# Alternating the C batches of a state-space layer between VectorE and GpSimd, with a second product buffer

## The chip, the cores and the metric

The kernel runs on one core of one Trainium2 chip. The metric is the device time of one execution in microseconds; of several runs the median is taken. The engines are TensorE (PE, with its weight loads PEld), VectorE (DVE), ScalarE (ACT), GpSimd (POOL) and SyncE (SP). SP, ACT and POOL can also start DMAs.

## The reference, cut to what matters

One layer of a trunk over 512 latent tokens (width 1024) with 256 context tokens. A normalised and modulated input goes through one wide projection, whose parts feed a short convolution (`xa`, `xb`, `cg`), a bidirectional S5 state-space layer (`u`) and a neighbourhood attention (`q`, `k`, `v`); sigmoid gates (`ga`, `gb`, `gc`) merge the three, and a squared-ReLU MLP follows. The change lies in the preparation of the state-space layer:

```python
lam_bar = jnp.exp(lam_dt)
b_bar = ((lam_bar - 1.0) / lam)[..., None] * lax.complex(b_re, b_im)
c_mat = lax.complex(c_re, c_im)
h_f = diag_scan(lam_bar[0], s5_drive(ux, b_bar[0])) + ...
y = jnp.real(einsum('blgp,gnp->blgn', h_f, c_mat[0]) + einsum('blgp,gnp->blgn', h_b, c_mat[1]))
```

The kernel runs the scan in chunks of 8 tokens. For that it needs the input matrices times the powers of `lam_bar` (called E here) and the output matrices times the powers of `lam_bar` (called CA here). Both are products of complex numbers, formed for 32 groups in 8 batches of 4 groups.

## The kernel before, in words

**The weights.** `UNITS` lists the work of TensorE: first `xa` 0 to 3, `cg` 0 to 3, `xb` 0 to 3, `uc` 0 to 3 (the context's part of `u`), then gates and the convolution's output, and so on to the MLP. `slot(i)` emits one unit. For it a weight block is loaded (`raw`, issued by SP), split into two parts that together hold float32 (`wh` by ScalarE at L173, `wl` by VectorE at L176), multiplied in 24 matmuls (L99 to L101, `mm3`), and evacuated from PSUM by `ev_unit` in the slot after. The PSUM tag `m` has three buffers, so an evacuation that is late stops TensorE some units later. The evacuation of `cg` is L950 to L953 (one ScalarE and five VectorE instructions), that of `xb` is L956 (VectorE, reads PSUM), L92 (ScalarE) and L93 (VectorE), that of `uc` is a ScalarE copy and two DMAs.

**The preparation beside it.** Each slot calls `pump()` twice, and `pump` advances every generator in `gens` by one step:

- `gen_s5e` forms E, all on GpSimd: for each batch `b` two times two products (`prod`, L422) and a sum (L458, L467). TensorE then uses the batch twice: `lags` multiplies it with C (tile `kps`), `turned` transposes it (tile `etps`); ScalarE copies the transposed batch to `et` (L445) and issues its DMA to `E_d` (L446). The batch's inputs `bc` are loaded by a DMA that ScalarE issues (L429).
- `gen_s5c` forms CA: for each batch four products (L422) and two sums (L499), then a DMA by SP to `C_d` (L501). The inputs `cb` (two buffers) are loaded by a DMA that ScalarE issues (L491). Batches 0 to 4 are VectorE's, 5 to 7 GpSimd's. `c1` (the result) and `tc` (the second product) have one buffer each, so a batch's first write of `c1` waits for the DMA of the batch before.

`gen_s5c` begins when the context's generator is done, and its pool takes the memory that the context used. When both preparations are emitted and the units have come to `ga`, these pools are given back, and `S5B` takes their memory: it loads `et`, `ca` and `ks` from DRAM and runs the scan on TensorE, VectorE, GpSimd and ScalarE between the gates' units.

**The order.** Each engine and each DMA queue runs its instructions in a fixed order. That order is laid out when the kernel is built, by a planner that goes by the program's order and by its own estimate of when each instruction could start; an instruction that waits holds everything behind it on its engine.

Of the kernel before, what the change touches and what calls it, by code (L numbers as in the profile page):

```python
# [9 lines left out]
F32 = mybir.dt.float32  # L10
# [65 lines left out]
def trunk(tc, xT, ctxT, cond, condT, vecs, wst, s5p, s5bc, dmat, biasA, outT):  # L76
# [3 lines left out]
    V, S, P, PE = nc.vector, nc.scalar, nc.gpsimd, nc.tensor  # L80
# [23 lines left out]
    with es:  # L104
# [11 lines left out]
        def pa(name):  # L116
            return pp.tile([128, 1024], F32, tag="a", bufs=2, name=name)
# [300 lines left out]
        def prod(eng, out, mat, cf, b):  # L418
            shp = [128, 4, 8, 16]
            m4 = mat[:, :, None, :].to_broadcast(shp)  # L420
            c4 = s5["CF"][cf][:, 4 * b:4 * b + 4, :, None].to_broadcast(shp)
            eng.tensor_tensor(out.rearrange("p (g s n) -> p g s n", g=4, s=8), m4, c4, op=MUL)  # L422

        def gen_s5e(pool):
            kev = pool.tile([128, 2, G, 16], F32, name="kev")

            def loadbc(b):
                t = pool.tile([128, 512], F32, tag="bc", bufs=2, name=f"bc{b}")
                nc.scalar.dma_start(t[:, 0:384], s5bc[b][:, 0:384])  # L429
                return t  # L430

            def lags(b, e1, cm):
                kps = pa(f"kps{b}")[:, :128].rearrange("p (g m) -> p g m", g=4)
                for g in range(4):
                    for c in range(2):
                        PE.matmul(kps[:, g], e1[:, c, 128 * g:128 * g + 128], cm[:, 4 * c + g], start=c == 0, stop=c == 1)
                S.copy(kev[:, :, 4 * b:4 * b + 4].rearrange("p e g m -> p g e m"), kps.rearrange("p g (e m) -> p g e m", e=2))

            def turned(b, e1):
                ps = pa(f"etps{b}").rearrange("p (a m) -> p a m", a=8)  # L440
                for g in range(4):
                    for c in range(2):
                        PE.transpose(ps[:, 2 * g + c], e1[:, c, 128 * g:128 * g + 128], ident)
                et = pool.tile([128, 8, 128], F32, tag="et", bufs=1, name=f"et{b}")
                S.copy(et, ps)  # L445
                nc.scalar.dma_start(E_d[b], et)  # L446

            bc, old = loadbc(0), None
            for b in range(9):
                if b < 8:  # L450
                    nxt = loadbc(b + 1) if b < 7 else None
                    B = bc[:, 0:128].rearrange("p (c g n) -> p c g n", c=2, g=4)
                    cm = bc[:, 128:384].rearrange("p (a m) -> p a m", a=8)
                    e1 = pool.tile([128, 2, 512], F32, tag="e1", bufs=2, name=f"e1{b}")
                    ta = pool.tile([128, 512], F32, tag="ta", name=f"ta{b}")
                    prod(P, e1[:, 0], B[:, 0], "cr", b)
                    prod(P, ta, B[:, 1], "nci", b)
                    P.tensor_tensor(e1[:, 0], e1[:, 0], ta, op=ADD)  # L458
                    yield
                if old is not None:  # L460
                    lags(b - 1, *old)
                    yield
                if b < 8:
                    ta = pool.tile([128, 512], F32, tag="ta", name=f"tb{b}")
                    prod(P, e1[:, 1], B[:, 0], "nci", b)
                    prod(P, ta, B[:, 1], "cr", b)
                    P.tensor_tensor(e1[:, 1], e1[:, 1], ta, op=SUB)  # L467
                    yield
                if old is not None:
                    turned(b - 1, old[0])  # L470
                    yield
                old = (e1, cm)
                bc = nxt

            kf0 = pool.tile([16, G, 16], F32, tag="bc", bufs=2, name="kf0")
            dmt = pool.tile([16, G, 16], F32, tag="bc", bufs=2, name="dmt")
            nc.scalar.dma_start(dmt, dmat)
            nc.sync.dma_start(kf0, kev[112:128, 0])
            yield
            V.tensor_tensor(kf0, kf0, dmt, op=ADD)  # L480
            V.tensor_tensor(kev[0:16, 1], kev[0:16, 1], kf0, op=ADD)
            for e, s in ((e, s) for s in range(8) for e in range(2) if e or s < 7):
                i = 16 * (7 * e + s)
                nc.sync.dma_start(KT_d[:, :, i:i + 16].rearrange("g n m -> n g m"), kev[16 * s:16 * s + 16, e])
            yield

        def gen_s5c(pool):
            for b in range(8):
                eng = V if b < 5 else P
                t = pool.tile([128, 128], F32, tag="cb", bufs=2, name=f"cb{b}")  # L490
                nc.scalar.dma_start(t, s5bc[b][:, 384:512])  # L491
                C = t.rearrange("p (c g n) -> p c g n", c=2, g=4)
                c1 = pool.tile([128, 2, 512], F32, tag="c1", bufs=1, name=f"c1{b}")
                yield
                for c, (x, y, o) in enumerate((("ar", "ai", SUB), ("ai", "ar", ADD))):
                    ta = pool.tile([128, 512], F32, tag="tc", name=f"tc{b}{c}")
                    prod(eng, c1[:, c], C[:, 0], x, b)
                    prod(eng, ta, C[:, 1], y, b)
                    eng.tensor_tensor(c1[:, c], c1[:, c], ta, op=o)  # L499
                    yield  # L500
                nc.sync.dma_start(C_d[b], c1)  # L501
                yield
# [654 lines left out]
        stc_cm.__exit__(None, None, None)  # L1157
        s5c_cm = tc.tile_pool(name="s5c", bufs=1, side="right")
        gcc = gen_s5c(s5c_cm.__enter__())
        gens.append(gcc)  # L1160
        while ga_ in gens or gcc in gens or UNITS[i][0] != "ga":
# [306 lines left out]
```

## Time and profile before

| what | value |
|---|---|
| runs | 1035.29, 1036.31, 1037.55 us |
| median | 1036.31 us |
| the profiled execution | 1036.69 us |
| its span, first to last instruction | 1034.9 us |
| mean granted TensorE clock | 0.979 |
| busy: PE, DVE, ACT, POOL | 995.7, 577.6, 379.9, 216.0 us |

The profiled execution is 1.8 us longer than its span. TensorE is busy for 96% of the span, and the other engines for at most 56%; the shares are means over stages that differ.

### The profile page before, as it was taken

The numbers are of one execution on the slowest core, as the hardware profiler recorded it, in microseconds if no ns is written. First come the engines' busy times: TensorE is split into PE (matmuls) and PEld (weight loads), VectorE is DVE, ScalarE is ACT, GpSimd is POOL, SyncE is SP. The second block draws the span as 40 slices with busy tenths as digits, with TensorE's granted clock in tenths as the row PEclk, the third lists the DMA queues.
The fourth block names the chain that finished last, engine by engine and source line by source line (L and its number), as shares of the span: only waits on it lengthen the run. The fifth ranks groups of instructions, "written<-read, shape, count | busy, mean of one in ns | idle before, by whom it ended". The sixth has DMA issues, their size and how long they took to land.

```text
span 1034.9 us, 13596 instructions
## 1 busy us (share of the span) xinstructions
PE 995.7 (96%) x5386; PEld 818.1 (79%) x5386; DVE 577.6 (56%) x941; ACT 379.9 (37%) x611; POOL 216.0 (21%) x169
## 2 busy tenths in 40 slices
PE   7999996999899999989999999999999999999997
PEld 4468886878788787878877788998888888888887
DVE  4943799468772145666487895665432324443322
ACT  3234522432222234555465443444321213442311
POOL 3165654657751023310210200000000000000000
PEclk8999998999899999999999999999999999999999
DMA  9427335973546465433344574223232232232202
GB/s 365 172 79 214 120 127 203 237 270 127 173 161 202 156 231 219 145 136 107 122 149 148 195 256 152 82 82 123 82 120 84 82 117 87 82 123 82 82 1 82
DMA packets 64543, 149.38 MB, mean 144 GB/s; under 512 B 28864, under 2 KB 41152, under 8 KB 52064
## 3 DMA queue, kind: packets, MB, share of 16 engines
q1 hardware_dynamic: 47360, 137.90, 38.8%
q10 hardware_dynamic: 17120, 10.62, 3.6%
q8 instruction: 42, 0.69, 0.3%
q14 instruction: 21, 0.17, 0.0%
HBM read 130.16 MB, written 18.32 MB: 143 GB/s over the span
## 4 chain that ended last, share of the span: by engine, by line
PE 66%; DVE 13%; DMA 8%; POOL 6%; issue 3%; ACT 3%; ACTq 0%; SPq 0%; DVEq 0%; POOLq 0%
PE m L99 10%; PE m L100 10%; PE m L101 10%; DMA raw<-in_wst_dram 4%; DVE wl L176 2%; PE ops L840 2%; DMA C_d<-c 2%; PE wo L100 1%; PE wo L99 1%; DVE v L689 1%; PE wo L101 1%; PE st_a L515 1%; DVE fg L953 1%; POOL junk L1086 1%; PE ptps L825 1%
## 5 line engine op out<-in xcount | busy, mean ns | idle before, releaser
L176 DVE TENSOR_TENSOR wl<-raw,wh 128x1024 fp32r<-128x1024 f32 x144 | 191.1, 1327 | 219.1 <-ACT wh L173 214.4
L173 ACT CAST wh<-raw 128x1024 fp32r<-128x1024 f32 x144 | 151.0, 1049 | 299.7 <-PE m L100 151.1
L99 PE MATMUL m<-rg,wh 128*128 128x512 f32 (+1 forms) x480 | 184.2, 385 | 0.0
L101 PE MATMUL m<-rg,wl 128*128 128x512 f32 (+1 forms) x480 | 183.9, 384 | 0.0
L101 PEld LDWEIGHTS m<-rg,wl 128*128 128x128 f32 x480 | 90.1, 188 | 19.1
L99 PEld LDWEIGHTS m<-rg,wh 128*128 128x128 f32 x480 | 89.9, 188 | 18.7
L100 PE MATMUL m<-rg,wh 128*128 128x512 f32 (+1 forms) x256 | 96.4, 378 | 0.0
L1086 POOL TENSOR_TENSOR junk<-raw,silx 128x1024 f32<-128x1024 f32 x16 | 45.9, 2868 | 208.6 <-DMA raw<-in_wst_dram 207.4
L100 PE MATMUL m<-actl,wh 128*128 128x512 f32 x224 | 87.8, 392 | 0.0
L100 PEld LDWEIGHTS m<-rg,wh 128*128 128x128 f32 x256 | 48.0, 188 | 8.6
L100 PEld LDWEIGHTS m<-actl,wh 128*128 128x128 f32 x224 | 42.0, 187 | 9.8
L1041 DVE SCALAR_TENSOR_TENSOR fg<-m,mod,fg 128x512 f32<-128x512 f32 x14 | 10.5, 751 | 52.8 <-PE m L101 52.8
L515 PE MATMUL st_a<-raw,cs 128*2 128x256 f32 x128 | 33.1, 415 | 4.9 <-DMA raw<-in_wst_dram 3.9
L689 DVE TENSOR_TENSOR_SCAN v<-r,v 128x96 f32<-128x96 f32 x64 | 29.5, 524 | 14.8 <-POOL v L681 14.8
L92 ACT CAST rg<-relu 128x512 fp32r<-128x512 f32 (+1 forms) x36 | 20.3, 575 | 38.5 <-DVE relu L1034 38.5
L1090 DVE SCALAR_TENSOR_TENSOR jk<-raw,silx 128x1024 bf16<-128x1024 f32 x16 | 21.8, 1361 | 20.5 <-DMA raw<-in_wst_dram 20.5
L93 DVE TENSOR_TENSOR actl<-relu,rg 128x512 fp32r<-128x512 f32 (+1 forms) x36 | 22.3, 631 | 18.5 <-ACT rg L92 18.5
L100 PE MATMUL wo<-rg,wh 128*128 128x256 f32 (+1 forms) x104 | 31.8, 309 | 0.0
L99 PE MATMUL wo<-rg,wh 128*128 128x256 f32 (+1 forms) x104 | 31.8, 307 | 0.0
L101 PE MATMUL wo<-rg,wl 128*128 128x256 f32 (+1 forms) x104 | 31.5, 306 | 0.0
L1087 ACT ACTIVATE junk<-junk 128x1024 f32<-128x1024 f32 x16 | 17.0, 1061 | 36.4 <-POOL junk L1086 36.4
L515 PEld LDWEIGHTS st_a<-raw,cs 128*2 128x2 f32 x128 | 10.8, 90 | 24.6 <-issue 10.8
(439 smaller groups left out, 2404.3 us busy)
## 6 DMA issues: line engine op xcount, KB each, us to landing
raw<-in_wst_dram SPq DMA_DIRECT2D x94, 1024.0 KB
E_d<-et ACTq DMA_DIRECT2D x8, 512.0 KB
C_d<-c SPq DMA_DIRECT2D x8, 512.0 KB
et<-E_d SPq DMA_DIRECT2D x8, 512.0 KB
ca<-C_d SPq DMA_DIRECT2D x8, 512.0 KB
raw<-in_wst_dram SPq DMA_DIRECT2D x4, 512.0 KB
u<-U_d SPq DMA_DIRECT2D x8, 256.0 KB
ks<-KT_d SPq DMA_DIRECT2D x32, 64.0 KB
```

Of the source, the lines that this page charges most:

```text
L92: S.copy(hi, src)
L93: (eng or V).tensor_tensor(lo, src, f(hi), op=SUB)
L99: PE.matmul(ps, a[0], b[0], start=start, stop=False)
L100: PE.matmul(ps, a[0], b[1], start=False, stop=False)
L101: PE.matmul(ps, a[1], b[0], start=False, stop=stop)
L173: S.copy(a, src)
L176: V.tensor_tensor(b, src, f(a), op=SUB)
L515: PE.matmul(ps, cs[:, kt], half(h)[:, 256 * (kt % 4):256 * (kt % 4) + 256], start=kt == 0, stop=kt == 7, skip_group_check=True)
L689: V.tensor_tensor_scan(v[:, g, c], r8, v[:, g, c], 0.0, op0=MUL, op1=ADD)
L840: PE.matmul(ops[r], v[:rows, vt, r], pt[:rows, h, t], start=t == 0, stop=t == 3, skip_group_check=True)
L1086: P.tensor_tensor(junk, half(h), silx, op=MUL)
L1090: V.scalar_tensor_tensor(jk, half(h), 1.0, silx, op0=MUL, op1=MUL, accum_out=modx[:, i:i + 1])
```

## The change

Three edits, all in the preparation of the state-space layer. Batch `b` of CA goes to GpSimd where `b` is odd and to VectorE where it is even, so that each has four. `c1` and `tc` have two buffers. `et` has two buffers.

```diff
@@ gen_s5e / turned
-                et = pool.tile([128, 8, 128], F32, tag="et", bufs=1, name=f"et{b}")
+                et = pool.tile([128, 8, 128], F32, tag="et", bufs=2, name=f"et{b}")
@@ gen_s5c
-                eng = V if b < 5 else P
+                eng = P if b % 2 else V
...
-                c1 = pool.tile([128, 2, 512], F32, tag="c1", bufs=1, name=f"c1{b}")
+                c1 = pool.tile([128, 2, 512], F32, tag="c1", bufs=2, name=f"c1{b}")
...
-                    ta = pool.tile([128, 512], F32, tag="tc", name=f"tc{b}{c}")
+                    ta = pool.tile([128, 512], F32, tag="tc", bufs=2, name=f"tc{b}{c}")
```

## Rows read from the trace of the kernel before

**Rows 1.** Three stretches of 26 us: busy us (and count) of PE, PEld, DVE, ACT, POOL; clock; DMA.
```profile
130.00:156.00 26.00, 26.00 (x140) 21.75 (x139) 25.89 (x32) 6.25 (x9) 13.54 (x10) 1.00 0.41 136
156.00:182.00 26.00, 18.07 (x109) 16.41 (x108) 23.72 (x27) 7.22 (x11) 11.10 (x8) 0.88 0.56 197
182.00:208.00 26.00, 25.71 (x137) 21.87 (x137) 11.18 (x10) 10.41 (x13) 16.22 (x14) 0.99 1.03 243
```

**Rows 2.** TensorE's waits, 156 to 182 us: total us, times, longest us.
```profile
PE etps L443 <- ACT et L445: 4.0, 1, 4.0
PE uc L99 <- DVE fg L956: 1.7, 1, 1.7
PE uc L101 <- DVE wl L176: 1.6, 1, 1.6
```

**Rows 3.** VectorE in time order: start us, us, instruction, idle before it.
```profile
156.92 1.49 DVE L422 TENSOR_TENSOR c<-cb,CFar 128x512 f32<-128x512 f32 x1 [1.00 <-DMA C_d<-c]
...
176.66 0.68 DVE L956 TENSOR_TENSOR fg<-xb,fg 128x512 f32<-128x512 f32 x1
177.26 0.68 DVE L499 TENSOR_TENSOR c<-c,tc 128x512 f32<-128x512 f32 x1
```

**Rows 4.** GpSimd in time order: E, its first CA batch, the scan's first instruction.
```profile
131.42 1.46 POOL L422 TENSOR_TENSOR tb<-bc,CFcr 128x512 f32<-128x512 f32 x1
...
140.72 1.06 POOL L422 TENSOR_TENSOR ta<-bc,CFnci 128x512 f32<-128x512 f32 x1 [6.14 <-DMA bc<-in_s5bc_dram]
...
156.80 1.05 POOL L422 TENSOR_TENSOR e<-bc,CFcr 128x512 f32<-128x512 f32 x1
157.82 1.50 POOL L422 TENSOR_TENSOR e<-bc,CFnci 128x512 f32<-128x512 f32 x1
...
162.55 1.61 POOL L467 TENSOR_TENSOR e<-e,tb 128x512 f32<-128x512 f32 x1
178.07 1.92 POOL L422 TENSOR_TENSOR tc<-cb,CFai 128x512 f32<-128x512 f32 x1 [13.92 <-ACT rg L92]
...
216.73 0.21 POOL L618 IOTA iot<- 128x96 int32 x1 [3.40 <-DMA C_d<-c]
```

**Rows 5.** Groups by form, 130 to 182 us: count, busy us, mean ns, idle before.
```profile
L499 DVE TENSOR_TENSOR c<-c,tc 128x512 f32<-128x512 f32 x10 | 8.4, 836 | 0.0
L953 DVE SCALAR_TENSOR_TENSOR fg<-fg,vec,fg 128x504 f32<-128x504 f32 x6 | 7.1, 1184 | 0.0
L422 DVE TENSOR_TENSOR c<-cb,CFai 128x512 f32<-128x512 f32 x5 | 6.5, 1290 | 0.0
L422 DVE TENSOR_TENSOR tc<-cb,CFai 128x512 f32<-128x512 f32 x5 | 4.3, 852 | 0.0
L422 DVE TENSOR_TENSOR c<-cb,CFar 128x512 f32<-128x512 f32 x5 | 4.2, 844 | 1.9 <-DMA C_d<-c 1.9
L422 DVE TENSOR_TENSOR tc<-cb,CFar 128x512 f32<-128x512 f32 x5 | 4.2, 835 | 0.1
L953 DVE SCALAR_TENSOR_TENSOR fg<-fg,vec,fg 128x7 f32<-128x7 f32 x6 | 3.9, 652 | 0.0
```

**Rows 6.** VectorE's L953, 130 to 182 us: ns min/median/max of one.
```profile
L953 DVE SCALAR_TENSOR_TENSOR fg<-fg,vec,fg x12: 210/876/1767, 128.7 to 150.3; 128x504 f32<-128x504 f32 x6, 128x7 f32<-128x7 f32 x6
```

**Rows 7.** ScalarE and its DMA issues in time order.
```profile
163.05 0.34 ACTq L491 DMA_DIRECT2D cb<-in_s5bc_dram  x1
...
177.90 1.01 ACT L445 COPY et<-etps 128x1024 f32<-128x1024 f32 x1
```

**Rows 8.** TensorE in time order: `kps` of the last E batch.
```profile
171.54 0.71 PE L436 MATMUL kps<-bc,e 128*128 128x32 f32 x5 [0.61 <-issue]
```

**Rows 9.** TensorE's waits, 216 to 230 us.
```profile
PE yps L711 <- DMA ks<-KT_d: 1.8, 1, 1.8
```

**Rows 10.** Busy time in stretches of 4 us; the granted clock is third from the end.
```profile
164.00:168.00 4.00, 2.35 (x12) 2.14 (x11) 3.63 (x5) 2.13 (x3) 0.15 (x1) 0.66 0.69 268
...
180.00:184.00 4.00, 4.00 (x27) 4.00 (x26) 1.67 (x2) 1.40 (x3) 3.19 (x3) 0.70 1.00 243
```

## What the change was expected to do

> **What bounds the kernel now.** I read the page first: TensorE is busy for 996 of 1035 us, so a change off TensorE can only win back, or add to, some 39 us of idle time and what the clock loses. I then asked for the busy time of every engine in stretches of 26 us, to find where that idle time lies beside the code that changes. The CA batches lie between 130 us, after which all five of VectorE's come, and 217 us, where the scan's first instruction had waited for the last of them [rows 4, 5]. From 130 to 156 us TensorE has no gap and VectorE is busy for 25.89 of 26 us; from 156 to 182 us TensorE is idle for 26.00 - 18.07 = 7.9 us while VectorE is busy for 23.7 [rows 1]. The view of TensorE's waits says on whom: 1.7 us for an evacuation of `xb` on VectorE, 1.6 us for a weight split on VectorE, 4.0 us for the copy of `et` on ScalarE [rows 2]. That copy starts at 177.90, right behind a cast that waits for the evacuation at 176.66 [rows 3, 7]. So all three, 7.3 us, are VectorE being late. I read its line in order of time to see why: the instructions of CA stand in front of the evacuations, and some take 1.49 us that elsewhere take 0.68 [rows 3].
>
> **Why those instructions are long.** VectorE starts a CA product at 156.92, GpSimd started a product at 156.80 that takes 1.05; VectorE's ends at 158.41, 0.56 after GpSimd's end at 157.85. GpSimd's next one starts at 157.82, takes 1.50 instead of 1.06, and ends 0.9 after VectorE's [rows 3, 4]. The two take turns, a whole instruction each. The evacuations L956, which read PSUM, keep their 0.68. The Trainium skill states this in "SBUF — State Buffer", section "Who interferes with whom": a VectorE instruction with two SBUF inputs contends with a GpSimd instruction that reads SBUF, and the one that comes second waits for the whole of the first. The trace agrees: 1.49 and 1.50 us against 0.68 and 1.06 alone. By that rule at its strictest, each us of GpSimd's work paid in full, the sum below would be 15.9 - 9.1 - 1.8 = +5.0 us, as an estimate; by the busy shares of the two engines alone it would be rival A's -10.4.
>
> What GpSimd's work costs VectorE can be read from the groups. From 130 to 182 us VectorE's 30 CA instructions take 8.4 + 6.5 + 4.3 + 4.2 + 4.2 = 27.6 us [rows 5]; at 0.68 each they would take 20.4, so 7.2 are waiting. The six long L953 take 7.1 against 6 x 0.68 = 4.1 (3.0 more), the six short ones 3.9 against 6 x 0.21 = 1.3 (2.6 more) [rows 5, 6]. Together 12.8 us. GpSimd ran 14 instructions of E against them (first at 131.42, last at 162.55), at least 14 x 1.06 = 14.8 us alone [rows 4]. Each us of GpSimd's work cost VectorE 12.8 / 14.8 = 0.86 us.
>
> **The change part by part.** *Batches 1 and 3 leave VectorE.* That takes 12 instructions of 0.60 (the distance of starts, 176.66 to 177.26 [rows 3]) from its line: 7.2 us. *The second buffer of `c1`* takes away VectorE's waits for the DMA to `C_d`: 1.9 us [rows 5]. Relief: 9.1 us.
>
> *The same batches come to GpSimd* while VectorE is still full. They can't start much earlier: their memory is the context's, and VectorE's five batches all come after 130 us [rows 5]. Two batches are 12 x 1.06 = 12.7 us, which at 0.86 cost VectorE 10.9 us. The bounds are 0 (GpSimd's part falls into VectorE's pauses) and 12.7; I take 0.86, since the rows are of the same engines, forms and stretch.
>
> *The second buffer of `tc`* frees batch 5. Before, GpSimd began it at 178.07, and the row names a ScalarE cast; but what ends just then is VectorE's last sum of batch 4 (177.26 + 0.68 = 177.94), which reads the only `tc` [rows 3, 4]. With two, batch 5 follows batch 3 on GpSimd and brings its 6.4 us forward. Bounds 0 and 6.4 us; I take half, 3.2, times 0.86: 2.7 us. Batch 6 moves to VectorE later, where that engine has room (11.2 of 26 us busy from 182 to 208 [rows 1]), and costs nothing.
>
> VectorE's balance by 178 us is thus -9.1 + 10.9 + 2.7 = +4.5 us later. TensorE already waits for it, so it is late by as much: +4.5 us, with bounds of -7.3 (its three waits gone; more can't be won there) and +10.0 (all 19.1 us of three batches paid).
>
> *Batches 5 to 7 in a row become 5 and 7.* The scan's memory comes free with the last DMA to `C_d`; GpSimd's first instruction of it waits until 216.73 [rows 4]. TensorE then waits 1.8 us for `ks`, loaded behind that [rows 9]. With one batch of 6.4 us less and no wait between batches this chain ends that much earlier, and TensorE comes later, so I take the whole 1.8 us off. Bounds: 0 and 1.8.
>
> *The second `et`* gives nothing: the copy that TensorE waited for stands behind the cast and so behind the evacuation of 176.66, not behind a busy buffer. If the buffer were the cause, at most the 4.0 us of [rows 2], already inside the 7.3.
>
> *Waits that the change adds.* ScalarE issues the load of `cb` for batch b + 2 once batch b has read its own; at 163.05 it issued one just as VectorE's last product of batch 2 ended [rows 7]. For odd batches it now waits for GpSimd, and behind it on ScalarE stand the casts `rg` and `wh` that VectorE and TensorE need. SP waits likewise with the DMA to `C_d` while weight loads stand behind it. I price both at 0, since GpSimd's batch ends at about the time of the next evacuation; if they bite, they add to the same lateness, up to the 6.4 us of one batch.
>
> *Clock.* TensorE's granted clock falls to 0.66 and 0.70 in slices after its gaps [rows 10], between its levels of 2.4 and 1.2 GHz. The gaps stay, so I leave it: 0. If they went, up to (0.34 + 0.30) x 4 = 2.6 us would come back.
>
> Sum: +4.5 - 1.8 = +2.7 us on the profiled execution's 1036.7 (span 1034.9 and 1.8 around it), 1039.4; the median of the runs is 0.4 lower, so **1039 us**. A difference under 0.2%, 2 us, can't be told from none.
>
> **The rivals.** *A, VectorE is freed (faster).* If GpSimd's batches fall into pauses (it waited 6.14 us for one load of `bc` [rows 4]), or the planner moves the evacuations ahead of CA, the 7.3 us go, 1.8 at the scan, and half of the clock's 2.6: 1036.3 - 10.4 = 1026 us. It decides where GpSimd's work costs VectorE less than s, with s x (12.7 + 3.2) = 9.1 + 1.8, s = 0.69. For it speaks that 0.69 is not far below 0.86; against it, that fewer VectorE instructions do not lessen what GpSimd demands.
>
> *B, nothing to be measured.* The overlap is near 0.69 and relief and cost cancel: 1036 us.
>
> *C, GpSimd's line holds up E (slower still).* The last E batch ends at 162.55 + 1.61 = 164.2 and TensorE needs it at 171.54 [rows 4, 8], 7.4 us later. If the planner puts batches 1 and 3 in front, 12.7 us and up to 12 turns of 0.60 for VectorE come before it, 19.9 us, of which the pause of 6.14 takes up some: 13.8 - 7.4 = 6.4 us late. That gives 1039 + 6 = 1045 us. It decides where more than 7.4 us are put in front; against it, the planner puts E's own instructions first in the program.
>
> **How the numbers follow.** My forecast (1037 to 1043) has 0.40, C 0.15, A 0.29, B 0.16. Slower is the forecast and C, 0.55; same is B, 0.16; faster is A, 0.29. The range leaves out a tenth on each side: down to 1027, into A, and up to 1048, where C and the unpaid waits on ScalarE meet. The likeliest case alone is 1037 to 1043.
>
> **What would show it.** Right: from 130 to 182 us VectorE's CA instructions still average above 0.8 us, GpSimd's busy time there rises from 24.6 to over 30 us, and TensorE's idle time from 156 to 190 us grows to over 10 us, its waits still on L956, L176 and L445. The wait for `ks` at 224 us is gone. Wrong: TensorE's idle time there is under 4 us (A), or its new wait is on `kps` (C). The forecast also fails if the planner's new order opens or closes gaps in the scan (from 216 us on), which I price at nothing.

## The result, and the profile after

The changed kernel takes 1047.74 us (median of 4 runs, 1043.79 to 1053.68); beside it on the same chip the kernel before took 1036.93 (4 runs, 1035.29 to 1037.98). The ratio is 1.0106, with a 95% interval from 1.0076 to 1.0136: slower by 10.8 us. The profiled execution of after took 1047.11 us with a span of 1045.3, which is 10.4 more than before.

**Where TensorE stands still.** The first fence is the view of busy time by stretch: the three stretches of [rows 1], then four of 4 us. The second is TensorE's waits, first from 124 to 212 us (total us, times, longest us), then from 208 to 345 us, where the scan lies.

```profile
130.00:156.00 26.00, 21.50 (x104) 17.01 (x104) 26.00 (x28) 4.37 (x6) 20.23 (x15) 0.92 0.28 104
156.00:182.00 26.00, 17.69 (x75) 14.52 (x74) 24.48 (x20) 6.49 (x10) 25.32 (x17) 0.76 0.55 197
182.00:208.00 26.00, 21.30 (x138) 20.20 (x138) 14.48 (x13) 9.47 (x14) 17.98 (x13) 0.86 0.82 229
...
172.00:176.00 4.00, 0.36 (x2) 0.37 (x2) 3.18 (x4) 1.20 (x2) 4.00 (x4) 0.56 0.24 91
176.00:180.00 4.00, 4.00 (x17) 3.78 (x17) 4.00 (x3) 0.75 (x3) 4.00 (x3) 0.50 0.37 108
196.00:200.00 4.00, 2.49 (x12) 2.49 (x12) 0.00 (x0) 0.00 (x0) 2.68 (x3) 0.54 0.98 182
200.00:204.00 4.00, 4.00 (x24) 4.00 (x24) 0.00 (x0) 1.28 (x2) 1.30 (x3) 0.60 0.88 283
```

```profile
PE kps L436 <- POOL e L467: 11.9, 3, 7.6
PE xb L101 <- DVE wl L176: 2.1, 1, 2.1
PE kps L436 <- POOL e L458: 2.0, 2, 1.2
PE xb L99 <- DVE fg L950: 1.6, 1, 1.6
...
PE stps L664 <- DMA u<-U_d: 3.9, 1, 3.9
PE yps L711 <- DMA ks<-KT_d: 2.7, 4, 1.1
PE yps L713 <- POOL h L703: 1.9, 1, 1.9
```

TensorE now waits 11.9 + 2.0 = 13.9 us for E at `kps`, where before it waited for nothing but its own sequencer [rows 8]. Its waits that lead back to VectorE went from 7.3 us [rows 2] to 2.1 + 1.6 = 3.7. So the new wait is on GpSimd: the two waits on VectorE lie at 150 and 153 us, and from 156 to 208 us all of TensorE's waits, 13.0 us, are at `kps`. In all TensorE is idle for 78 - 60.49 = 17.5 us of these three stretches; before it was 8.2. The clock is the second part of the loss: in the slices after a standstill TensorE is busy all the time at a granted clock of 0.50 (which is 1.2 of 2.4 GHz) or 0.60.

**Why E is late.** GpSimd in time order (start, us, instruction, idle before it), then the two batches of `kps` on TensorE that waited longest:

```profile
127.51 1.32 POOL L422 TENSOR_TENSOR c<-cb,CFar 128x512 f32<-128x512 f32 x1 [3.65 <-DMA cb<-in_s5bc_dram]
128.79 1.49 POOL L422 TENSOR_TENSOR c<-cb,CFai 128x512 f32<-128x512 f32 x1
130.25 1.58 POOL L422 TENSOR_TENSOR e<-bc,CFcr 128x512 f32<-128x512 f32 x1
...
170.95 1.50 POOL L422 TENSOR_TENSOR c<-cb,CFar 128x512 f32<-128x512 f32 x1
172.41 1.50 POOL L422 TENSOR_TENSOR c<-cb,CFai 128x512 f32<-128x512 f32 x1
173.87 1.71 POOL L467 TENSOR_TENSOR e<-e,tb 128x512 f32<-128x512 f32 x1
...
196.20 1.26 POOL L467 TENSOR_TENSOR e<-e,tb 128x512 f32<-128x512 f32 x1
197.42 1.26 POOL L499 TENSOR_TENSOR c<-c,tc 128x512 f32<-128x512 f32 x1
202.53 0.21 POOL L618 IOTA iot<- 128x96 int32 x1 [3.85 <-DMA C_d<-c]
```

```profile
175.63 3.19 PE L436 MATMUL kps<-bc,e 128*128 128x32 f32 x14 [7.57 <-POOL e L467]
...
197.51 3.20 PE L436 MATMUL kps<-bc,e 128*128 128x32 f32 x14 [3.46 <-POOL e L467]
```

The first write of `c`, which is batch 1 of CA, starts at 127.51, ahead of all but the first product of E's last three batches. The last sum of E ends at 196.20 + 1.26 = 197.46, against 164.16 before [rows 4]: 33.3 us later. All 24 CA instructions of batches 1, 3, 5 and 7 lie between 127.51 and 198.68, 23 of them ahead of that last sum. And what took 1.06 us alone now takes some 1.5: in this stretch GpSimd and VectorE both have full queues of instructions that read SBUF, and take turns.

**VectorE.** Groups by form, 130 to 182 us (count, busy us, mean ns), beside [rows 5]; then two of its lines in time order:

```profile
L499 DVE TENSOR_TENSOR c<-c,tc 128x512 f32<-128x512 f32 x7 | 7.8, 1115 | 0.0
L422 DVE TENSOR_TENSOR c<-cb,CFai 128x512 f32<-128x512 f32 x4 | 6.4, 1600 | 0.0
L422 DVE TENSOR_TENSOR tc<-cb,CFai 128x512 f32<-128x512 f32 x4 | 6.4, 1598 | 0.0
L422 DVE TENSOR_TENSOR c<-cb,CFar 128x512 f32<-128x512 f32 x4 | 3.7, 922 | 0.7 <-DMA C_d<-c 0.7
L422 DVE TENSOR_TENSOR tc<-cb,CFar 128x512 f32<-128x512 f32 x3 | 3.1, 1046 | 0.0
```

```profile
184.01 1.43 DVE L499 TENSOR_TENSOR c<-c,tc 128x512 f32<-128x512 f32 x1
185.36 0.68 DVE L956 TENSOR_TENSOR fg<-xb,fg 128x512 f32<-128x512 f32 x1
```

VectorE does 22 CA instructions in 27.4 us, where it did 30 in 27.6: the mean went from 0.92 to 1.25. Taking eight instructions off it in this stretch freed nothing. Its last evacuation of `xb` starts 8.7 us later than before (185.36 against 176.66 [rows 3]), with no idle time in front of it. TensorE shows no wait for it: it has just stood still longer at `kps`.

**The whole span.** The first matmul of `ga`, in the kernel before and then in after:

```profile
188.63 0.40 PE L99 MATMUL ga<-rg,wh 128*128 128x512 f32 x1
204.11 0.40 PE L99 MATMUL ga<-rg,wh 128*128 128x512 f32 x1
```

It starts 15.5 us later. The scan's first matmul is 7.4 later (228.5 against 221.1), `q` 14.9, `wo` 10.4, the end 10.4. The same is seen in a ledger worked out from the view of busy time in stretches of 26 us: idle time is the stretch less TensorE's busy time; what the clock took is the busy time times (1 - granted clock), an estimate. For after, from 130 to 208 us, that is 21.50 x 0.08 + 17.69 x 0.24 + 21.30 x 0.14 = 8.9 us.

| idle + clock, us | 0 to 130 | 130 to 208 | 208 to 338 | 338 to 650 | sum |
|---|---|---|---|---|---|
| before | 9.2 + 5.7 | 8.2 + 2.4 | 6.9 + 6.4 | 8.8 + 3.3 | 50.9 |
| after | 9.4 + 4.4 | 17.5 + 8.9 | 8.7 + 4.2 | 5.6 + 1.8 | 60.5 |

The difference, 9.6 us, is close to the 10.4 of the span. From 130 to 208 us 15.8 us are lost, 9.3 as idle time and 6.5 by the clock; 1.1 are won ahead of it, 0.4 in the scan and 4.7 from 338 to 650 us, where gates and attention lie. From 650 us on both lose alike: nothing up to 1014 us, and some 6 us of idle time behind that. These are two single executions: E7 below, whose edit is worth nothing, has 6.8 + 0.0 from 338 to 650 us in its profile, 5.3 less than before, so the 4.7 won there can't be told from chance.

### The profile page after: what moved, and what is told of

It is laid out like the page before. It is cut to its first block, busy times and chain, and to the rows that moved or that the text cites. A ratio compares the mean times of both kernels' runs of the same rounds, so it can differ in the third digit from the quotient of the medians.

```text
span 1045.3 us, 13591 instructions
## 1 busy us (share of the span) xinstructions
PE 998.1 (95%) x5386; PEld 820.2 (78%) x5386; DVE 586.6 (56%) x935; ACT 378.8 (36%) x610; POOL 229.2 (22%) x175
## 4 chain that ended last, share of the span: by engine, by line
PE 72%; DVE 13%; POOL 6%; DMA 5%; ACT 3%; issue 2%; SPq 0%; ACTq 0%; DVEq 0%; POOLq 0%
PE m L99 10%; PE m L100 10%; PE m L101 10%; DMA raw<-in_wst_dram 3%; DVE wl L176 2%; DVE v L689 2%; PE ops L840 2%; PE wo L100 1%; PE wo L99 1%; PE wo L101 1%; PE gc L100 1%; PE gc L99 1%; PE gc L101 1%; PE gb L100 1%; PE gb L99 1%
## 5 line engine op out<-in xcount | busy, mean ns | idle before, releaser
L176 DVE TENSOR_TENSOR wl<-raw,wh 128x1024 fp32r<-128x1024 f32 x144 | 191.8, 1332 | 234.8 <-ACT wh L173 225.6
L436 PEld LDWEIGHTS kps<-bc,e 128*128 128x128 f32 x128 | 23.0, 221 | 17.3 <-POOL e L467 12.8
L1090 DVE SCALAR_TENSOR_TENSOR jk<-raw,silx 128x1024 bf16<-128x1024 f32 x16 | 23.9, 1497 | 20.6 <-DMA raw<-in_wst_dram 20.5
L436 PE MATMUL kps<-bc,e 128*128 128x32 f32 x128 | 20.9, 281 | 13.9 <-POOL e L467 11.9
```

Source lines behind the costliest of these rows:

```text
L176: V.tensor_tensor(b, src, f(a), op=SUB)
L1090: V.scalar_tensor_tensor(jk, half(h), 1.0, silx, op0=MUL, op1=MUL, accum_out=modx[:, i:i + 1])
```

## The experiments

All were compared with the kernel before on the same chip. Single runs of the kernel before spread from 1030.9 to 1044.2 us, so a profile, which is one execution, can stand some us off its kernel's median. The profiles of E3, E7 and E8 are the shortest of their ten runs, those of E1 and E4 the longest of ten, that of E12 the longest of four. The ratio is worked out from the single runs and is not the quotient of the two medians. In E4, E5 and E9 to E12 the added lines move later line numbers by one to five (the sums of L499 are L500, L503 or L504 there).

| | kernel | median us (runs) | before us (runs) | ratio, 95% interval |
|---|---|---|---|---|
| E1 | alternation alone | 1039.99 (10) | 1037.13 (31) | 1.0022, 1.0001 to 1.0042 |
| E2 | second buffers alone | 1038.56 (10) | same | 1.0020, 0.9999 to 1.0041 |
| E3 | after, all batches on VectorE | 1036.05 (10) | same | 0.9997, 0.9977 to 1.0017 |
| E4 | after, E ahead on GpSimd | 1036.98 (10) | same | 1.0010, 0.9986 to 1.0034 |
| E5 | after, GpSimd's CA without reads | 1036.85 (10) | 1036.76 (25) | 0.9993, 0.9965 to 1.0021 |
| E8 | before, second `c1` | 1039.95 (10) | same | 1.0037, 1.0009 to 1.0066 |
| E9 | after, CA emitted late | 1036.51 (10) | same | 0.9989, 0.9965 to 1.0012 |
| E10 | before, CA emitted late | 1018.85 (4) | same | 0.9813, 0.9781 to 0.9846 |
| E6 | after, `tc` for each engine | 1053.56 (4) | 1036.56 (19) | 1.0158, 1.0078 to 1.0238 |
| E7 | before, second `et` | 1039.47 (10) | same | 1.0001, 0.9968 to 1.0035 |
| E11 | E10 with second buffers | 1034.43 (10) | same | 0.9978, 0.9947 to 1.0009 |
| E12 | E10 with alternation | 1025.76 (4) | same | 0.9889, 0.9823 to 0.9956 |

### E1, E2 and E3: the parts alone

E1 keeps the alternation and takes back the buffers:

```diff
-                c1 = pool.tile([128, 2, 512], F32, tag="c1", bufs=2, name=f"c1{b}")
+                c1 = pool.tile([128, 2, 512], F32, tag="c1", bufs=1, name=f"c1{b}")
...
-                    ta = pool.tile([128, 512], F32, tag="tc", bufs=2, name=f"tc{b}{c}")
+                    ta = pool.tile([128, 512], F32, tag="tc", name=f"tc{b}{c}")
...
-                et = pool.tile([128, 8, 128], F32, tag="et", bufs=2, name=f"et{b}")
+                et = pool.tile([128, 8, 128], F32, tag="et", bufs=1, name=f"et{b}")
```

> Only the alternation; c1, tc and et keep one buffer. Theory G (the CA batches stand between E's instructions on GpSimd, so the last E batch, whose end moved from 164 to 197 us, comes late and TensorE waits for it at kps): two CA batches still come before the end of E, so E ends near 180 us, TensorE waits some 5 us at kps, and the time is 1041 to 1046 us. Theory V (the turns with GpSimd make VectorE late, and TensorE waits for its evacuations and weight splits): the batches wait for each other's DMA, fewer of them overlap, and the time is 1037 to 1041 us with the waits on L950, L956 and L176.

E2 keeps the buffers and takes back the engines:

```diff
-                eng = P if b % 2 else V
+                eng = V if b < 5 else P
```

> Only the second buffers of c1, tc and et; the engines stay as before (batches 0 to 4 VectorE, 5 to 7 GpSimd). Theory G: GpSimd's CA comes at the end of E's line, E ends near 165 us, kps does not wait, and the time is that of before or less, 1033 to 1037 us. Theory V: no CA of GpSimd stands against VectorE before 164 us, the DMA waits of 1.9 us are gone, so also 1033 to 1037 us. If it is slower than 1040 us, the buffers and not the alternation are the cause and both theories fall.

E3 keeps the buffers and gives GpSimd no CA at all:

```diff
-                eng = P if b % 2 else V
+                eng = V
```

> All eight CA batches on VectorE, with the second buffers. GpSimd has E alone. Theory G: E ends near 165 us, TensorE does not wait at kps, and the time is within 3 us of before, 1034 to 1040 us. Theory V: VectorE takes 18 instructions of 0.60 us more, but fewer turns; its line is late by up to 10 us at the uc units, but the excess over 0.68 us of a CA instruction is only that of E; the time is 1036 to 1044 us with waits on L956 and L176 alone.

Measured: 1.0022, 1.0020 and 0.9997. Each half of the change costs about 0.2% (E2's interval just takes in 1), both together 1.06%, so most of the loss belongs to the two in combination. Two expectations failed: E1's time lies where theory V had it, under G's 1041, though its wait is G's; and in E2 both theories had no wait at `kps` and 1037 us at most. TensorE's waits at `kps` from 124 to 212 us, E1 and then E2:

```profile
PE kps L436 <- POOL e L467: 8.0, 2, 6.2
```

```profile
PE kps L436 <- POOL e L467: 3.2, 1, 3.2
...
PE kps L436 <- POOL tc L422: 2.1, 1, 2.1
```

E's last sum ends at 178.0 in E1, 186.3 in E2, 197.5 in after and 170.8 in E3. With one `c1`, a batch of CA waits for the DMA of the batch before it, on whichever engine that was; this brake holds GpSimd's batches back so that E gets through: 9 CA instructions stand ahead of E's last sum in E1, 7 in E2, 23 in after. With two and the engines of before, only batches 5 to 7 are there to be pulled forward; with both changes, four batches without a brake. E3 has no CA on GpSimd, no wait for GpSimd at `kps`, 48 instructions on VectorE instead of 30, and the time of before: that VectorE carries CA is not what costs. The profile of E1 is the slowest of its ten runs, so its 8.0 us may be at the upper end.

The second buffers have a price of their own on VectorE. From 130 to 156 us E2, E3 and E4 stand still for 4.3 to 4.5 us, as after does, most of it for VectorE's `cg` evacuation and weight split; before, E1 and E7, with one `c1`, have no gap there, and E5 below, with memsets, has none either. This part of the loss is VectorE's, and E3 and E4 have the time of before in spite of it.

### E7, E8 and E6: the buffers one by one

E7 gives the kernel before the second `et`, E8 the second `c1`:

```diff
-                et = pool.tile([128, 8, 128], F32, tag="et", bufs=1, name=f"et{b}")
+                et = pool.tile([128, 8, 128], F32, tag="et", bufs=2, name=f"et{b}")
```

```diff
-                c1 = pool.tile([128, 2, 512], F32, tag="c1", bufs=1, name=f"c1{b}")
+                c1 = pool.tile([128, 2, 512], F32, tag="c1", bufs=2, name=f"c1{b}")
```

> The kernel before with one edit: et has two buffers. Both theories and the prediction: nothing, 1035 to 1038 us.

> The kernel before with one edit: c1 has two buffers. Theory B (the single buffer kept the planner from putting the next batch in front of the evacuations; with two, CA crowds ahead of L950 and L176): TensorE gets a gap of 3 to 5 us between 130 and 156 us, where it had none, kps does not wait, and the first ga unit starts 3 to 8 us later than the 188.6 of before; by the runs so far 2 to 4 us of that last to the end: 1037 to 1041 us. Rival: the buffer only takes away the DMA waits of 1.9 us, and the time is 1034 to 1037 us.

E7 measured 1.0001: the second `et` is worth nothing (the median is 1.5 us above the range expected, but the interval takes in 1), and TensorE's longest wait is still 3.9 us for that copy. E8 measured 1.0037: the second `c1` alone costs about what E2 does, within their intervals. So the 1.9 us that VectorE waits for the DMA to `C_d` are not a gain to be had. How E8 loses is not shown; its profile, the fastest of its ten runs, has a wait for GpSimd at `kps` (two CA instructions stand ahead of E's last sum, which ends at 176.4) and a long one for `ks` in the scan:

```profile
PE kps L436 <- POOL e L467: 2.9, 1, 2.9
PE yps L711 <- DMA ks<-KT_d: 8.2, 1, 8.2
```

The time is as theory B had it, but not the place: from 130 to 156 us TensorE stands still for 1.4 us, not 3 to 5, and `kps` does wait.

E6 gives each engine its own pair of `tc`, in after, so that GpSimd no longer waits for VectorE's sums and the reverse:

```diff
-                    ta = pool.tile([128, 512], F32, tag="tc", bufs=2, name=f"tc{b}{c}")
+                    ta = pool.tile([128, 512], F32, tag=f"tc{b % 2}", bufs=2, name=f"tc{b}{c}")
```

> The changed kernel, but even and odd batches have tc tiles of their own (two each). In the changed kernel GpSimd's products wait 8.4 us in all for VectorE's sums, which read the shared tc. If that coupling is a large part of E's lateness, E ends 5 us or more earlier than 197 us, the first ga unit starts before 200 us, and the time is 1040 to 1045 us; if CA's instructions between E's and their turns are the cause by themselves, E ends within 3 us of 197 us and the time is 1044 to 1050 us.

Measured 1.0158, with an interval that overlaps that of after; 1053.56 us is above both ranges that were expected. It doesn't mend anything: GpSimd's waits for VectorE's sums are gone (5.2 us in after by the view of waits, not the 8.4 of the expectation), but E's last sum ends at 199.8, and the waits at `kps` come to 16.2 us. The shared `tc` is not what makes E late.

### E4 and E5: taking the suspected cause away

E4 is after with E's instructions ahead on GpSimd: the even batches are emitted first, and each instruction of an odd batch is ordered behind E's last sum (`order["elast"]`, set in `gen_s5e`).

```diff
-            for b in range(8):
+            for b in (0, 2, 4, 6, 1, 3, 5, 7):
                 eng = P if b % 2 else V
+                if b == 1:
+                    for _ in range(4):
+                        yield
...
+                    with after("elast" if b % 2 else None):
```

> The changed kernel, but the batches come in the order 0, 2, 4, 6, 1, 3, 5, 7, and the odd ones are queued on GpSimd behind E's last instruction. Theory G: kps does not wait, E ends near 165 us, and most of the loss is back: 1034 to 1039 us. Theory V: VectorE's turns with CA come after 165 us instead of before, where its last evacuations of xb still lie, so half of the loss stays: 1039 to 1044 us, with waits on L956 and L176 after 165 us.

Measured 1036.98 us, 1.0010: the loss is gone (the profiled execution, 1043.56, is the slowest of its ten). The profile shows the order on GpSimd, E's last sum and then the first product of CA:

```profile
172.20 1.62 POOL L467 TENSOR_TENSOR e<-e,tb 128x512 f32<-128x512 f32 x1
173.78 2.04 POOL L422 TENSOR_TENSOR c<-cb,CFar 128x512 f32<-128x512 f32 x1
```

This also moves the turns: VectorE's last CA instruction starts at 164.6, ahead of GpSimd's first, so E4 does not tell the place in the queue from the turns. TensorE's waits from 124 to 212 us hold no `kps`; the longest is again the one of before:

```profile
PE etps L443 <- ACT et L445: 3.4, 1, 3.4
```

E5 is after with the odd batches' products and sums left out, so that these parts of CA are not computed; two memsets of the same tile stand in place of each, 48 in all.

```diff
+                    if b % 2:
+                        for out in (c1[:, c], ta, c1[:, c]):
+                            P.memset(out, 0.0)
+                            P.memset(out, 0.0)
+                    else:
+                        prod(eng, c1[:, c], C[:, 0], x, b)
+                        prod(eng, ta, C[:, 1], y, b)
+                        eng.tensor_tensor(c1[:, c], c1[:, c], ta, op=o)
```

> The changed kernel, but in the odd batches each of GpSimd's products and sums is left out and two memsets of the same tile stand in its place (0.52 us each in the trace of before for 128x512), so GpSimd's line is as long without turns but its instructions read nothing from SBUF. Theory V (turns): VectorE's CA, L953, L176 and L93 lose the waits against CA and keep only those against E; TensorE's waits on L950 and L176 go, and the time is 1035 to 1040 us. Theory G (E is held up by what stands between its instructions): E still ends after 180 us, TensorE still waits at kps for 5 us or more, and the time is 1041 to 1046 us.

Measured 1036.85 us, 0.9993. Groups by form on GpSimd and VectorE, 124 to 200 us:

```profile
L499 POOL MEMSET tc<- 128x512 f32 x8 | 4.2, 525 | 6.5 <-DVE c L504 6.5
L422 POOL TENSOR_TENSOR e<-bc,CFnci 128x512 f32<-128x512 f32 x3 | 4.5, 1500 | 0.0
...
L504 DVE TENSOR_TENSOR c<-c,tc 128x512 f32<-128x512 f32 x8 | 8.2, 1033 | 0.0
```

E's last sum on GpSimd and TensorE's longest wait, 124 to 212 us:

```profile
175.59 1.31 POOL L467 TENSOR_TENSOR e<-e,tb 128x512 f32<-128x512 f32 x1
PE kps L436 <- POOL e L467: 4.6, 1, 4.6
```

E still stands behind memsets, 44 of the 48, but its last sum ends at 176.9 instead of 197.5 and TensorE waits 4.6 us at `kps` instead of 13.9. The time is theory V's, and G's 1041 to 1046 did not come: CA's place alone, without reads that take turns and at this length, does not cost the 10.8 us. A memset keeps 0.525 us beside a full VectorE, while one form of E's products, which read, still takes 1.50. E5 takes two things away at once, the reads and some of the length (the 48 memsets are 24.4 us busy; the 24 CA instructions of after are 38.3 in the same view), so how much each is worth is not told apart. The profile is 3.2 us ahead of before at `ga` (185.4) and 2.0 at the end; idle time from 208 to 338 us is 10.3 us instead of 6.9, where E7, whose edit is worth nothing, has 9.4.

### E9 to E12: CA emitted later

If the place of CA in the queues is the cause, it should help to put it where VectorE and GpSimd are free. E9 (on after) and E10 (on before) begin CA at the first unit of `uc`, at double rate; VectorE's part is ordered behind the evacuations of `xb`, GpSimd's behind E's last sum.

```diff
-        gens.append(gcc)
+        rate[gcc] = 2
         while ga_ in gens or gcc in gens or UNITS[i][0] != "ga":
+            if UNITS[i] == ("uc", 0):
+                gens.append(gcc)
             slot(i)
...
+                    with after("xb" if eng is V else "elast"):
```

> The changed kernel with CA emitted from the first uc unit on at double rate; VectorE's batches are queued behind the evacuation of xb, GpSimd's behind E's last instruction. If CA's place in the two lines is the whole cause, TensorE has under 2 us of gaps between 130 and 190 us, the first ga unit starts at 178 to 184 us (188.6 before, 204.1 with the change), and the time is 1023 to 1031 us. If the turns or the engines themselves are the cause, the loss moves to the uc and ga units and the time is 1036 us or more.

> The kernel before (batches 0 to 4 VectorE, 5 to 7 GpSimd, single buffers) with the same late emission and queueing. If the place in the lines is the cause, 1023 to 1032 us, as the run with the alternation, within 3 us; if the alternation and the buffers help once they are out of the way, it is slower than that run by more than 3 us, since its batches wait for each other's DMA and the scan begins later.

E9 comes back to the time of before, 1036.51 us, not to the 1023 to 1031 that was expected if the place were all. E10 beats both kernels and its own range: 1018.85 us, 1.9% less than before. Its busy time by stretch, then GpSimd and VectorE's sums (groups, 150 to 215 us):

```profile
130.00:156.00 26.00, 26.00 (x140) 21.75 (x139) 18.86 (x23) 9.25 (x13) 16.74 (x13) 1.00 0.38 137
156.00:182.00 26.00, 26.00 (x186) 24.36 (x185) 20.41 (x24) 8.76 (x14) 5.62 (x4) 1.00 0.74 202
182.00:208.00 26.00, 25.78 (x114) 21.02 (x113) 15.78 (x21) 9.82 (x12) 0.00 (x0) 1.00 0.90 256
```

```profile
159.63 2.15 POOL L467 TENSOR_TENSOR e<-e,tb 128x512 f32<-128x512 f32 x1
211.71 1.06 POOL L422 TENSOR_TENSOR tc<-cb,CFai 128x512 f32<-128x512 f32 x1 [49.94 <-DVE c L500]
```

```profile
L500 DVE TENSOR_TENSOR c<-c,tc 128x512 f32<-128x512 f32 x10 | 6.9, 686 | 0.1
```

All but the first few of VectorE's CA instructions now run while GpSimd is idle, the sums are back at 0.69 us, and TensorE has next to no gap (0.2 us of 78) and keeps the full clock. E9 has the same front, with `ga` at 175.6, but loses the lead in the scan. TensorE's waits of E9, 208 to 345 us:

```profile
PE yps L712 <- DMA ks<-KT_d: 4.9, 3, 2.7
PE stps L665 <- DMA u<-U_d: 4.3, 2, 3.5
PE yps L714 <- POOL h L704: 2.8, 1, 2.8
```

E11 and E12 tell apart what E9 has and E10 has not: E11 is E10 with second buffers for `c1`, `tc` and `et`, E12 is E10 with the alternation (`eng = P if b % 2 else V`).

> Late emission and queueing as in the two late runs, engines as before (0 to 4 VectorE, 5 to 7 GpSimd), with the change's second buffers. Theory S (the buffers let the planner count CA as done earlier, so it puts the scan's first matmul behind only 197 matmuls of gates instead of 331, earlier than its data is there, and TensorE waits in the scan): 1032 to 1039 us, as the late run with the alternation and the buffers. Rival (the alternation is what costs the 18 us between the two late runs): 1017 to 1023 us.

> Late emission and queueing, the alternation, but single buffers for c1, tc and et; the planner puts 319 matmuls of gates before the first of the scan. Theory S: 1016 to 1024 us, as the late run with the engines and buffers of before. Rival (the alternation costs): 1032 us or more.

The ledger of these kernels, as above:

| idle + clock, us | `ga` first | gates ahead of the scan | 130 to 208 | 208 to 338 | 338 to 650 |
|---|---|---|---|---|---|
| before | 188.6 | 139 | 8.2 + 2.4 | 6.9 + 6.4 | 8.8 + 3.3 |
| E9, alternation and buffers | 175.6 | 195 | 3.7 + 1.7 | 12.5 + 8.9 | 8.5 + 5.0 |
| E11, buffers | 177.5 | 197 | 3.4 + 1.6 | 12.5 + 7.3 | 5.9 + 3.3 |
| E12, alternation | 178.1 | 319 | 0.9 + 0.0 | 10.6 + 7.6 | 7.3 + 1.6 |
| E10, neither | 177.6 | 331 | 0.2 + 0.0 | 5.1 + 7.6 | 4.5 + 1.7 |

The third column counts the matmuls of gates and of the convolution's output that stand ahead of the scan's first matmul in TensorE's recorded order. At late emission the second buffers cost 0.9978 - 0.9813 = 1.65 hundredths without the alternation (E11 against E10) and 1.0 with it (E9 against E12); the alternation costs 0.8 without the buffers and next to nothing with them. With the buffers CA is done sooner (GpSimd's first instruction of the scan starts at 222.2 in E9 and 225.0 in E11, in E10 at 247.5), and the planner puts the scan on TensorE after 195 or 197 such matmuls; the scan then starts at 225.8 and 228.6 and its idle time is 12.5 us. With one buffer it starts at 253.2 behind 331, in E10 with 5.1 us idle. The scan's place alone does not fit the five rows: before starts it behind 139 matmuls with 6.9 us idle, E12 at 251.8 behind 319 with 10.6, and E12's time of 1025.76 us is above the 1016 to 1024 that theory S gave. The scan was not moved by itself, so what the buffers cost at late emission is measured, and how is open. E10's gain is 10.4 us from 130 to 208, 0.6 in the scan and 5.9 from 338 to 650 us; the last is close to the 5.3 that E7's profile has in that stretch without a gain in time.

## Why the prediction was right, and where it was not

**The direction was right, the size was not.** The forecast was +2.7 us, the result +10.8. At 1047.74 the median lies within the range by 0.3 us; it left the likeliest case's own range of 1037 to 1043 and went past rival C's 1045. That it fell inside is luck, and the sign came out by rival C's path. Of the signs, VectorE's CA instructions (1.25 us) and GpSimd's busy time (45.6 us) came; TensorE's idle time from 156 to 190 us is 9.6 us, short of 10, its waits there are not on L956, L176 or L445, and the wait for `ks` stayed. The sign of C, a new wait on `kps`, came.

**The step that failed** is the place of the lateness: "VectorE's balance by 178 us is thus [...] +4.5 us later. TensorE already waits for it, so it is late by as much." VectorE's line did become late, by 8.7 us at the last evacuation of `xb`, but TensorE's waits on VectorE fell to 3.7 us, all ahead of 156 us. The wait that decided is rival C's, on `kps`, 13.9 us. The argument against C, that "the planner puts E's own instructions first in the program", fell: the planner put CA ahead of E's last three batches and between their instructions. E3 and E4 show that CA of GpSimd ahead of E is needed for the loss: without it the time is that of before. E5 shows that it is not enough by itself: with memsets in these places the time is that of before too. How much the place and how much the turns are worth was not told apart.

**C itself was sized too small.** It counted batches 1 and 3, 12 instructions, in front; all four odd batches were, 23 of 24 instructions. It had E 6.4 us late past its slack of 7.4; E ended 33.3 us later, which is 25.9 past the slack. TensorE's idle time in the three stretches of [rows 1] grew by only 9.3: the waits on VectorE became shorter, and the lateness is spread over five waits at `kps` with other work of TensorE between them (`uc` starts at 180.1, between the two long ones).

**The rate of 0.86** was the first term to be wrong. By the same working for after, 130 to 182 us: VectorE's 22 CA instructions took 27.4 us instead of 22 x 0.68 = 15.0, and its L953 5.0 us more than alone, 17.4 in all, against 31 instructions of GpSimd, 31 x 1.06 = 32.9 us. That is 0.53, an estimate. The rest is paid by GpSimd: it too waits for its turn, some 1.5 us for one of 1.06, and this stretching of GpSimd's own line had no term in the sum. By the Trainium skill, "SBUF — State Buffer", section "Who interferes with whom", the instruction that comes second waits for the whole of the first; the trace agrees in both directions here, 1.60 for 0.68 and 1.50 for 1.06. The same section has it that a GpSimd instruction that only writes does not contend, and E5's memsets of 0.525 us agree.

**The clock** was priced at 0 because the gaps were expected to stay, although the forecast itself had them grow. They grew, and the clock took 8.9 us instead of 2.4 of these stretches: 6.5 us, the largest term that was missing. The ledger has both sizes: 9.3 + 6.5 = 15.8 us by 208, and `ga` is 15.5 late.

**The relief was mis-sized.** The 7.2 us for two batches off VectorE did not come. The 1.9 us for DMA waits shrank only to 0.7, and E8 has a second `c1` as a loss. **The scan:** the wait for `ks` did not go; it is 2.7 us in four parts beside 3.9 for `u`, together 6.6 where before had 5.2, though GpSimd's first instruction of the scan came 14.2 us earlier (202.53 against 216.73 [rows 4]). The -1.8 was wrong. **Nothing for `et`** was right (E7). **The added waits** for `cb` and `C_d`, priced at 0, were 3.7 us on GpSimd for `cb` at 127.5, with E's instructions standing behind; how much of that reached TensorE was not told apart.

**Not foreseen:** 6.2 of the 15.8 us are won outside the stretch, most of it from 338 to 650 us. One part of that is named by the waits: TensorE's wait for `pr` at `ptps` is 2.9 us before and 0.3 after. In E7 it is 1.4, so part of it at least is the difference between two executions; whether the later start causes the rest was not tried.

## What to carry to other kernels

Before moving work to an engine that has time by its busy share, ask what stands in that engine's queue with a consumer waiting, and how many of the moved instructions will come in between; here that was E, with 7.4 us of slack against 24 instructions. A single buffer can act as a brake that keeps less urgent work out of a busy stretch: taking it away cost time in three places (after against E1, E8 against before, E11 against E10). Where two engines slow each other by turns, moving one's work to another time was worth more than sharing it out: the same instructions on the same engines, emitted later, gave 1.9%. That held with single buffers and the engines of before; with second buffers the same move gave nothing that could be told from none.

## What the runs showed of the hardware that was not expected

Taking turns lengthens both engines when both queues are full: in after, from 130 to 182 us, a VectorE product of 128 x 512 float32 takes 1.60 us on average for the two `CFai` forms and a GpSimd one 1.3 to 1.9 by its form, against 0.68 and 1.06 alone. A GpSimd memset of the same size keeps 0.525 us in E5 beside a full VectorE. A standstill of TensorE cost more than its own length: 9.3 us more idle time came with 6.5 us more lost to the granted clock, an estimate, which was 0.50 in the 4 us after the wait of 7.57 us, although TensorE was busy all through them.
